# Head 1's second and third attention groups as block products, with another way of splitting the first plain weights

## The chip, the cores and the metric

The kernel runs on one core of a Trainium2 chip. The metric is the time of one execution on the device in microseconds (us). Five queues of instructions matter: TensorE (PE, matrix products, with its weight loads PEld), VectorE (DVE), ScalarE (ACT), GpSimd (POOL) and SyncE (SP). SP and POOL issue the transfers (DMAs) here.

## The reference

The reference is a trunk of two layers on a sequence of 512 tokens with 1024 channels, in float32. Layer 0 mixes tokens by attention, layer 1 by causal pooling, and each is followed by a SwiGLU network with 2816 hidden channels. The change touches the attention layer alone:

```
qkv = (rmsnorm(x) @ w_qkv).reshape(B, S, 3 groups, 3 (q, k, v), 8 heads, 128)
for g, (window, dil) in enumerate(((128, 1), (512, 4), (2048, 16))):
    o[g], lse[g] = dilated_window_attention(q[g], k[g], v[g], window, dil, slopes[g])
o = sum over g of softmax(lse over g)[g] * o[g]
x = x + o.reshape(B, S, 1024) @ w_out
```

Each head therefore needs, for each of three groups, a q and a k: two products of a 1024x128 weight with the 1024x512 normalized input.

## The kernel before, in words

**Products in split precision.** Every float32 operand is split into a high part (rounded to the type that PE takes) and a low part (what is left). A product is the sum of three: high x high, high x low, low x high. `split` (line 90) makes the two parts: ACT writes the high part (L91), then DVE subtracts it from the raw value and writes the low part (L92).

**Two kinds of product.** The plain kind (`Product`, L312, L313 and L315 in this order for each of 8 slices of the contraction) gives one 128x512 result from 24 matmuls that stream 512 columns. L315 is the one that needs the weight's low part. The block kind (`seven`, L444 to L446 inside `mult`) gives two results, q and k of a group, at once: both operands are cut into 2x2 blocks, and 7 block products take the place of 8. Each block product is 12 matmuls that stream 256 columns, so a pair takes 84. It needs sums of weight blocks (`Pair`: the raw blocks come by three transfers on SP, a fourth on POOL, L159, adds one block to two others on the way, and DVE adds twice more, L175 and L176), sums of input blocks (T), and sums of the results (L485, L493, L498, L499 on DVE).

**The input blocks T** are made by `prepare(k)` for k = 0 to 3, between the early products: two multiplications (L561), three subtractions or additions (L565, L566, L570) and four splits of 512 columns each.

**Weights and their order.** A list of loads and a list of splits are filled at the start, in the order in which the weights are used. `pump` is called after each product and takes the next load if raw tiles are free (4 of them; `prepare` takes two of them as well) and the next split if a weight tile (5 of them, each with a high and a low half) is free. So at most five split weights stand ahead of PE. The first units after the four products of the prologue (L905) are here called:

- U0, U1: q and k of group 2 of head 0;
- U2, U3: v of group 0 for heads 0 and 1;
- U4, U5: q and k of group 0 of head 1;
- U6 to U9: q and k of groups 1 and 2 of head 1.

All ten are plain in the kernel before. Heads 2 to 7 use block products throughout. After head 1's groups comes `values12` (L615 to L617), a block product for the values of groups 1 and 2.

**What stands around U0.** After the prologue's products the program computes the norm's factor: PE sums squares (L394), DVE scales (L397), POOL takes a power (L400), PE spreads the result (L407), ACT copies it out as `row` (L914). Three eighths of U0's product are written before the spread and the rest behind it. The program text is not the order in the queues: a scheduler goes through the text and gives each engine its instructions in the order in which it reckons them to be ready, earlier text first.

**Between head 1's groups.** After group 0 comes `merge` of head 0; after group 2 come `turn0`, `turn12` (transposes of head 0's weights, L782 and L803, with copies) and `scores0` of head 1 (L699).

Of the kernel before, what the change touches and what calls it, by code (L numbers as in the profile page):

```python
# [8 lines left out]
F32 = mybir.dt.float32  # L9
F32R = mybir.dt.float32r  # L10
AF = mybir.ActivationFunctionType
OP = mybir.AluOpType
# [24 lines left out]
NF = 4  # L37
# [1 line left out]
K2 = KC // 2  # L39
NPLAIN = 4  # L40
WARM = 6
NSOLO = 3
PARTS = {0: ((0, 6, False), (6, 14, True), (14, 22, True)), 1: ((0, 2, False), (2, 10, True), (10, 18, True), (18, 22, False))}
ENDS = 5
BACK = {"blocks": 3, "sums": 7}
# [14 lines left out]
QK = [(0, 0), (0, 1), (1, 0), (1, 1), (2, 0), (2, 1)]  # L60
# [4 lines left out]
def trunk(ctx: ExitStack, tc: tile.TileContext, xT, xN, norms, w_first, w_qk, w_qkp, w_v0, w_v0p, w_v12, w_out, w_pair, w_down, w_dblock, w_pin, w_pgrp,  # L65
          consts, ident_in, invcnt_in, outT, outR):
    nc = tc.nc
# [22 lines left out]
    def split(hi, lo, v):  # L90
        nc.scalar.activation(hi, v, AF.Copy)  # L91
        nc.vector.tensor_tensor(lo, v, hi.bitcast(F32), op=OP.subtract)  # L92
# [7 lines left out]
    class Held:  # L100


        def __init__(self, ring, shift=0):
            self.live = True
            n = COLS[ring]
            if ring in ("w", "half"):
                t = wpool.tile([P, 2 * n + LINE], F32R, tag=ring, name=ring, bufs=BUFS[ring])
                self.t = [t[:, shift + i * n:shift + (i + 1) * n] for i in range(2)]
            else:
                self.t = wpool.tile([P, n], F32, tag=ring, name=ring, bufs=BUFS[ring])  # L110
            rings[ring].append(self)
# [8 lines left out]
    class Plain:  # L120


        def __init__(self, *srcs, shift=0):
            self.srcs, self.n, self.w, self.shift = srcs, sum(src.shape[-1] for src in srcs), None, shift
            loads.append((self, {"raw": 1}, self.load))
            steps.append((self, "w", self.split))

# [6 lines left out]

        def split(self):
            self.w = Held("w", self.shift)
            split(*(t[:, :self.n] for t in self.w.t), self.raw.t[:, :self.n])
            self.raw.done()

    class Pair:  # L140
# [68 lines left out]
            steps.extend(parts)  # L209
        units.append((these,))  # L210

    def share(n, *srcs, shift=0):
        unit = Plain(*srcs, shift=shift)
        each = unit.n // n
        units.extend([(unit, i * each, each, i == n - 1) for i in range(n)])

# [2 lines left out]
        share(1, src[:, S:3 * S])  # L219
        share(1, src[:, 3 * S:], src[:, :S])  # L220

    def plain(*srcs):
        for src in srcs:
            share(1, src)

    for h in range(HEADS):
        if h == 0:
            plain(*[w_qk[u] for u in range(len(QK) - NF)])
        for g in range(3):
            if h == 1 and g < NSOLO:  # L230
                plain(*[w_qk[len(QK) - NF + 2 * g + c] for c in range(2)])
            elif h:
                pairs(w_qkp[3 * h - 3 - NSOLO + g])
        if h == 0:
            plain(w_v0[0], w_v0[1])
        elif h % 2 == 0:
            pairs(w_v0p[h // 2 - 1])
        else:
            pairs(w_v12[h // 2, 0], w_v12[h // 2, 1], shift=APART)
# [343 lines left out]
    with tc.tile_pool(name="opool", bufs=1) as opool:  # L583
        early = opool.tile([P, HEADS, S], F32R, tag="o", name="early")
        with tc.tile_pool(name="apool", bufs=1) as apool:
# [253 lines left out]
            H, T, o = {}, {}, []  # L839
# [46 lines left out]
            for k in range(KC):  # L886
# [15 lines left out]
                for j, (w, v) in enumerate(((hi, 0), (hi, 1), (lo, 0))):  # L902
                    for i, f in enumerate(lead):
                        c = (k % 2 * NF + i) * P
# [43 lines left out]
            for h in range(1, HEADS):  # L948
                for g in range(3):
                    if h == 1 and g < NSOLO:  # L950
                        for c in range(2):
# [58 lines left out]
    with tc.tile_pool(name="fpool", bufs=2) as fpool:  # L1010
# [326 lines left out]
        t = total(late, add(0, 1, f))  # L1337
        t = total(t, add(1, 1, end(1, 1, range(HALF))))
# [5 lines left out]
        t = total(t, add(2, 1, end(2, 1, range(HALF // 2, HALF), f)))  # L1344
# [3 lines left out]
        t = total(t, add(3, 1, f))  # L1348
# [101 lines left out]
```

## Time and profile before

| what | value |
|---|---|
| median of three runs | 1194.25 us (1193.57 to 1194.67) |
| the profiled execution's own time | 1194.79 us |
| its span, first to last instruction | 1192.6 us |
| PE busy | 1182.2 us (99%) |
| DVE busy | 995.0 us (83%) |
| ACT busy | 680.8 us (57%) |
| POOL busy | 147.5 us (12%) |
| granted PE clock | 0.998 |

The profiled execution is 0.54 us above the median. An engine's busy time counts an instruction from its start to its end; consecutive instructions of one engine may overlap a little, so the distance between two starts is often shorter than the duration given. Idle time of an engine is put down to the instruction whose end came last before it went on. In the chain that ended last, each piece is a stretch of time, so its length is the distance from one piece to the next.

### The profile page before, as it was taken

The numbers are of one execution on the slowest core, as the hardware profiler recorded it, in microseconds if no ns is written. First come the engines' busy times: TensorE is split into PE (matmuls) and PEld (weight loads), VectorE is DVE, ScalarE is ACT, GpSimd is POOL, SyncE is SP. The second block draws the span as 40 slices with busy tenths as digits, with TensorE's granted clock in tenths as the row PEclk, the third lists the DMA queues.
The fourth block names the chain that finished last, engine by engine and source line by source line (L and its number), as shares of the span: only waits on it lengthen the run. The fifth ranks groups of instructions, "written<-read, shape, count | busy, mean of one in ns | idle before, by whom it ended". The sixth has DMA issues, their size and how long they took to land.

```text
span 1192.6 us, 24834 instructions
## 1 busy us (share of the span) xinstructions
PE 1182.2 (99%) x9936; PEld 1120.0 (94%) x9936; DVE 995.0 (83%) x1712; ACT 680.8 (57%) x1214; POOL 147.5 (12%) x137
## 2 busy tenths in 40 slices
PE   9999999999999999999999999999999999999997
PEld 7889999999999988898999999998789999999997
DVE  6978898889788856795799889997989998898875
ACT  6445564555456544562677567763455776676553
POOL 1111211111111000101111111100310111111100
PEclk9999999999999999999999999999999999999999
DMA  8346656665766534336677777753153777777732
GB/s 285 118 107 159 158 152 161 171 159 149 189 146 163 158 140 126 88 110 161 160 198 190 187 200 197 192 176 124 54 123 91 192 196 200 197 187 196 193 89 71
DMA packets 73363, 188.40 MB, mean 158 GB/s; under 512 B 7312, under 2 KB 9504, under 8 KB 73248
## 3 DMA queue, kind: packets, MB, share of 16 engines
q1 hardware_dynamic: 50400, 141.98, 35.2%
q0 software_dynamic: 22704, 44.58, 23.2%
q8 instruction: 77, 1.26, 0.4%
q14 instruction: 38, 0.31, 0.1%
q10 hardware_dynamic: 144, 0.26, 0.1%
HBM read 184.70 MB, written 2.10 MB: 157 GB/s over the span
## 4 chain that ended last, share of the span: by engine, by line
PE 91%; DVE 5%; issue 2%; ACT 1%; DMA 0%; POOL 0%; DVEq 0%; POOLq 0%; SPq 0%; ACTq 0%
PE ps L444 19%; PE ps L445 18%; PE ps L446 18%; PE ps L312 7%; PE ps L313 7%; PE ps L315 7%; PE ps L615 2%; PE ps L617 2%; PE ps L616 2%; PE ps L905 2%; DVE w L92 2%; PE ps L827 1%; PE ps L699 1%; DVE far L92 1%; PE ps L821 1%
## 5 line engine op out<-in xcount | busy, mean ns | idle before, releaser
L91 ACT ACTIVATE w<-raw 128x1024 fp32r<-128x1024 f32 (+1 forms) x299 | 313.6, 1056 | 211.7 <-PE ps L446 69.0
L92 DVE TENSOR_TENSOR w<-raw,w 128x1024 fp32r<-128x1024 f32 (+1 forms) x299 | 361.7, 1214 | 59.0 <-ACT w L91 55.3
L444 PE MATMUL ps<-far,w 128*128 128x256 f32 x916 | 251.9, 275 | 0.1
L445 PE MATMUL ps<-far,w 128*128 128x256 f32 x916 | 252.0, 275 | 0.0
L446 PE MATMUL ps<-far,w 128*128 128x256 f32 x916 | 251.8, 275 | 0.0
L444 PE MATMUL ps<-near,w 128*128 128x256 f32 x632 | 178.5, 282 | 0.4 <-ACT first L526 0.4
L445 PE MATMUL ps<-near,w 128*128 128x256 f32 x632 | 174.8, 277 | 0.0
L446 PE MATMUL ps<-near,w 128*128 128x256 f32 x632 | 174.8, 277 | 0.0
L444 PEld LDWEIGHTS ps<-far,w 128*128 128x128 f32 x916 | 171.8, 188 | 0.6 <-ACT first L526 0.5
L445 PEld LDWEIGHTS ps<-far,w 128*128 128x128 f32 x916 | 172.0, 188 | 0.2
L446 PEld LDWEIGHTS ps<-far,w 128*128 128x128 f32 x916 | 172.0, 188 | 0.0
L444 PEld LDWEIGHTS ps<-near,w 128*128 128x128 f32 x632 | 118.9, 188 | 1.3 <-ACT first L526 0.9
L445 PEld LDWEIGHTS ps<-near,w 128*128 128x128 f32 x632 | 118.8, 188 | 0.0
L446 PEld LDWEIGHTS ps<-near,w 128*128 128x128 f32 x632 | 118.8, 188 | 0.0
L313 PE MATMUL ps<-near,w 128*128 128x512 f32 (+1 forms) x284 | 106.4, 375 | 1.3 <-DVE near L377 1.3
L312 PE MATMUL ps<-near,w 128*128 128x512 f32 (+1 forms) x284 | 107.0, 377 | 0.0
L315 PE MATMUL ps<-near,w 128*128 128x512 f32 (+1 forms) x284 | 106.2, 374 | 0.0
L159 POOL DMA_DIRECT2D raw<-w_pair x36 | 43.7, 1213 | 361.5 <-DMA raw<-w_pair 135.1
L313 PEld LDWEIGHTS ps<-near,w 128*128 128x128 f32 x284 | 53.4, 188 | 11.4 <-DVE near L377 2.1
L312 PEld LDWEIGHTS ps<-near,w 128*128 128x128 f32 x284 | 53.4, 188 | 9.4
L315 PEld LDWEIGHTS ps<-near,w 128*128 128x128 f32 x284 | 53.3, 188 | 9.5
L91 ACT ACTIVATE half<-rawhalf 128x512 fp32r<-128x512 f32 x81 | 51.0, 631 | 14.7 <-PE ps L446 12.5
(319 smaller groups left out, 2731.2 us busy)
## 6 DMA issues: line engine op xcount, KB each, us to landing
raw<-w_pair SPq DMA_DIRECT2D x80, 512.0 KB, 4.4
raw<-w_qkp SPq DMA_DIRECT2D x36, 512.0 KB, 4.2
raw<-w_pair POOLq DMA_DIRECT2D x36, 512.0 KB, 7.4
raw<-w_dblock SPq DMA_DIRECT2D x32, 512.0 KB, 4.3
raw<-w_v SPq DMA_DIRECT2D x18, 512.0 KB, 4.1
raw<-w_qkp POOLq DMA_DIRECT2D x18, 512.0 KB, 7.3
rawhalf<-w_pair SPq DMA_DIRECT2D x36, 256.0 KB, 5.0
raw<-w_dblock POOLq DMA_DIRECT2D x16, 512.0 KB, 7.5
```

The lines of the kernel that those rows point to most:

```text
L91: nc.scalar.activation(hi, v, AF.Copy)
L92: nc.vector.tensor_tensor(lo, v, hi.bitcast(F32), op=OP.subtract)
L159: nc.gpsimd.dma_start(self.b.rearrange("p (a c) -> p a c", a=2), self.src[:, None, 3 * n:].to_broadcast([P, 2, n]), accum_op=OP.add)
L312: nc.tensor.matmul(self.p[:, cols], w[0][:, s], mh[:, cols], start=self.done == 0, stop=False)
L313: nc.tensor.matmul(self.p[:, cols], w[0][:, s], ml[:, cols], start=False, stop=False)
L315: nc.tensor.matmul(self.p[:, cols], w[1][:, s], mh[:, cols], start=False, stop=self.done == self.n)
L444: nc.tensor.matmul(dst, w.t[0][:, c], th, start=k == 0 and not on, stop=False, skip_group_check=on)
L445: nc.tensor.matmul(dst, w.t[0][:, c], tl, start=False, stop=False, skip_group_check=on)
L446: nc.tensor.matmul(dst, w.t[1][:, c], th, start=False, stop=k == n - 1, skip_group_check=on)
L615: nc.tensor.matmul(o, mh, wh, start=k == 0, stop=False)
L616: nc.tensor.matmul(o, mh, wl, start=False, stop=False)
L617: nc.tensor.matmul(o, ml, wh, start=False, stop=k == K2 - 1)
```

## The change

Three constants and conditions are edited.

- `NSOLO` goes from 3 to 1. Of head 1, only group 0 stays a pair of plain products; groups 1 and 2 become block products (`seven`), whose weights come as two `Pair` units (here P6 and P7) in place of the plain units U6 to U9. What was written after group 2 (`turn0`, `turn12`, `scores0`) is handed to `seven`, which issues it behind its first, third and fifth block product.
- Units U0 to U5 are `lean`: ACT writes the high part as before and then its negative into the low tile, and a transfer issued by POOL adds the raw weight from memory to it. DVE has no part in these splits, and the raw tile is free once ACT has read it.
- The weights on the host's side are laid out to fit (`w_qk` shorter, `w_qkp` longer), through the same constant.

```
-NSOLO = 3
+NSOLO = 1
...
     class Plain:
-        def __init__(self, *srcs, shift=0):
-            self.srcs, self.n, self.w, self.shift = srcs, sum(src.shape[-1] for src in srcs), None, shift
+        def __init__(self, *srcs, shift=0, lean=False):
+            self.srcs, self.n, self.w, self.shift, self.lean = srcs, sum(src.shape[-1] for src in srcs), None, shift, lean
             loads.append((self, {"raw": 1}, self.load))
             steps.append((self, "w", self.split))
...
         def split(self):
             self.w = Held("w", self.shift)
-            split(*(t[:, :self.n] for t in self.w.t), self.raw.t[:, :self.n])
+            hi, lo = (t[:, :self.n] for t in self.w.t)
+            if self.lean:
+                nc.scalar.activation(hi, self.raw.t[:, :self.n], AF.Copy)
+                nc.scalar.activation(lo, hi.bitcast(F32), AF.Copy, scale=-1.0)
+                o = 0
+                for src in self.srcs:
+                    nc.gpsimd.dma_start(lo[:, o:o + src.shape[-1]], src.bitcast(F32R), accum_op=OP.add)
+                    o += src.shape[-1]
+            else:
+                split(hi, lo, self.raw.t[:, :self.n])
             self.raw.done()
...
     for h in range(HEADS):
         if h == 0:
-            plain(*[w_qk[u] for u in range(len(QK) - NF)])
+            plain(*[w_qk[u] for u in range(len(QK) - NF)], lean=True)
         for g in range(3):
             if h == 1 and g < NSOLO:
-                plain(*[w_qk[len(QK) - NF + 2 * g + c] for c in range(2)])
+                plain(*[w_qk[len(QK) - NF + 2 * g + c] for c in range(2)], lean=True)
             elif h:
                 pairs(w_qkp[3 * h - 3 - NSOLO + g])
         if h == 0:
-            plain(w_v0[0], w_v0[1])
+            plain(w_v0[0], w_v0[1], lean=True)
```

`plain` and `share` pass `lean` on. The loop that uses it stands unchanged:

```
if h == 1 and g < NSOLO:
    for c in range(2):
        evac(h, 2 * g + c, product(0))
    for fs in between(h, g).values():
        for f in fs:
            f()
else:
    ...
    seven(T, QKV[h, g, 0], QKV[h, g, 1], scratch, between(h, g), g == 0)
```

More of the change, by code (lines that the diff above doesn't have):

```diff
@@ L210, in pairs, with share @@
         units.append((these,))
-    def share(n, *srcs, shift=0):
-        unit = Plain(*srcs, shift=shift)
+    def share(n, *srcs, shift=0, lean=False):
+        unit = Plain(*srcs, shift=shift, lean=lean)
         each = unit.n // n
@@ L220, in plain_gu, with plain @@
         share(1, src[:, 3 * S:], src[:, :S])
-    def plain(*srcs):
+    def plain(*srcs, lean=False):
         for src in srcs:
-            share(1, src)
+            share(1, src, lean=lean)
     for h in range(HEADS):
         if h == 0:
-            plain(*[w_qk[u] for u in range(len(QK) - NF)])
+            plain(*[w_qk[u] for u in range(len(QK) - NF)], lean=True)
         for g in range(3):
             if h == 1 and g < NSOLO:
-                plain(*[w_qk[len(QK) - NF + 2 * g + c] for c in range(2)])
+                plain(*[w_qk[len(QK) - NF + 2 * g + c] for c in range(2)], lean=True)
             elif h:
```

## The prediction

> **What bounds the kernel now.** I read the page's first and fourth parts, then the stages by windows, then the queues around the places of the change.
>
> ```profile
> PE 1182.2 (99%) x9936; PEld 1120.0 (94%) x9936; DVE 995.0 (83%) x1712; ACT 680.8 (57%) x1214; POOL 147.5 (12%) x137
> ...
> PE 91%; DVE 5%; issue 2%; ACT 1%; DMA 0%; POOL 0%; DVEq 0%; POOLq 0%; SPq 0%; ACTq 0%
> ```
>
> PE is busy for 99% of the span and holds 91% of the chain that ended last. So PE work taken out shortens the kernel one for one, as long as no wait takes its place, and any wait put into PE's row costs its length. DVE at 83% is the engine that could become late.
>
> The stretch that is replaced, in the chain that ended last (start, length, what):
>
> ```profile
> 66.88 0.29 PE ps L312
> ...
> 88.48 0.23 PE ps L315
> 88.71 0.44 PE ps L782 x4
> ...
> 90.88 0.32 PE ps L615
> 91.20 0.12 PE ps L616
> ```
>
> Between 66.88 and 88.71 PE does nothing but the four plain products of head 1's groups 1 and 2: 96 matmuls in 21.83 us, 0.2274 us each. No wait stands in it.
>
> Three stretches by windows (from and to, length, then busy time and count for PE, PEld, DVE, ACT, POOL):
>
> ```profile
> 200.00:220.00 20.00, 20.00 (x179) 20.00 (x178) 16.34 (x21) 10.10 (x17) 1.77 (x2) 1.00 0.78 190
> 34.00:67.00 33.00, 33.00 (x267) 27.48 (x266) 30.64 (x52) 17.45 (x38) 2.41 (x2) 1.00 0.34 97
> 67.00:88.00 21.00, 21.00 (x94) 17.40 (x93) 16.84 (x33) 7.38 (x12) 3.72 (x4) 1.00 0.44 115
> ```
>
> From 200 to 220 block products run without a gap: 179 matmuls in 20 us, 0.1117 us each, with the weight loads busy all the time. From 34 to 67, just ahead of the change, DVE is busy for 30.64 of 33 us; from 67 to 88, where the plain products are, for 16.84 of 21.
>
> **The change part by part.**
>
> **Block products for groups 1 and 2.** They remove 96 long matmuls (21.83 us) and add 2 x 84 short ones: 168 x 0.1117 = 18.77 us. Gain: 3.06 us. The moved insertions (two sets of transposes and the scores) hold the same matmuls as before, but PE now goes back to products three times, not once. After the scores the first product's piece took 0.32 us where the next took 0.12, so a return costs about 0.2 us; two more cost between 0 and 0.4 us. I take 0.1, since the transposes (0.44 us for four) are more like the products than the scores are, and a row for that return is not shown. The gain is then 2.95, with ends of 2.66 and 3.06.
>
> **What DVE gets for it.** Rows of the first 300 us by shape:
>
> ```profile
> L92 DVE TENSOR_TENSOR w<-raw,w 128x1024 fp32r<-128x1024 f32 x69 | 83.7, 1221 | 15.9 <-ACT w L91 15.2
> L175 DVE TENSOR_TENSOR raw<-raw 128x512 f32<-128x512 f32 x20 | 13.7, 687 | 1.6 <-DVE w L92 1.0 <-DVE qk L499 0.5
> L176 DVE TENSOR_TENSOR raw<-raw 128x512 f32<-128x512 f32 x20 | 13.7, 685 | 0.1
> L92 DVE TENSOR_TENSOR half<-rawhalf,half 128x512 fp32r<-128x512 f32 x20 | 13.7, 685 | 0.0
> L498 DVE TENSOR_TENSOR qk<-ps,sums 128x512 f32<-128x512 f32 x12 | 8.2, 685 | 0.0
> L485 DVE TENSOR_TENSOR qk<-ps,first 128x512 f32<-128x512 f32 x12 | 8.1, 677 | 0.0
> L593 DVE TENSOR_TENSOR qk<-ps,row 128x512 f32<-128x512 f32 x12 | 8.1, 685 | 1.5 <-PE ps L315 1.4
> ...
> L493 DVE TENSOR_TENSOR sums<-ps,qk 128x512 f32<-128x512 f32 x8 | 5.5, 685 | 0.2
> L499 DVE TENSOR_TENSOR qk<-sums,ps 128x256 f32<-128x256 f32 x12 | 4.9, 412 | 0.0
> ```
>
> A block pair's weights cost DVE 3 x 1.22 + 0.69 for splits and 2 x 0.69 for additions, 5.7 us; its results cost 0.68 + 0.69 + 0.69 + 0.41 = 2.5. A plain group costs 2 x 1.22 + 2 x 0.69 = 3.8. Each exchanged group adds 4.4 us, both 8.8. The lean units take away one 1.22 each, 7.3 in all, but not where the work is added: U0 to U4 were split before 34 us, so the crowded stretch gets back U5's alone.
>
> First test, the input blocks T. The rows of DVE in order of time (U5 to U9, then the last splits of `prepare(3)`):
>
> ```profile
> 37.81 1.22 DVE L92 TENSOR_TENSOR w<-raw,w 128x1024 fp32r<-128x1024 f32 x1
> ...
> 42.29 1.23 DVE L92 TENSOR_TENSOR w<-raw,w 128x1024 fp32r<-128x1024 f32 x1
> ...
> 49.64 1.22 DVE L92 TENSOR_TENSOR w<-raw,w 128x1024 fp32r<-128x1024 f32 x1
> ...
> 55.11 1.22 DVE L92 TENSOR_TENSOR w<-raw,w 128x1024 fp32r<-128x1024 f32 x1
> ...
> 62.64 1.23 DVE L92 TENSOR_TENSOR w<-raw,w 128x1024 fp32r<-128x1024 f32 x1 [0.51 <-ACT w L91]
> ...
> 69.28 0.68 DVE L92 TENSOR_TENSOR h<-raw,h 128x512 fp32r<-128x512 f32 x1
> ...
> 72.89 0.68 DVE L92 TENSOR_TENSOR tx<-raw,tx 128x512 fp32r<-128x512 f32 x1
> ```
>
> In the kernel before T is whole at 73.57, long ahead of its first use at 90.88. Now group 1 starts near 66.9 and its fourth block product wants the last piece 45 matmuls later, at 66.88 + 45 x 0.1117 = 71.9. To be done by then, from 34 on: the 30.64 of before, less five splits (6.1), plus P6's weights (5.7), plus P7's first split (1.2), plus the part of `prepare(3)` that ran after 67 (four splits and two more operations of some 0.7 us, one multiplication, two short additions: about 5 us). That is 36.4, so the end lies at 70.4 if DVE never idles, and at 72.8 with the 2.4 us of idle time that the stretch had. The raw tiles set that idle time, and a lean unit gives its tile back after ACT instead of after DVE, so some of it should go. PE would wait between 0 and 0.9 us; with T no earlier than before, 1.7. I take 0.3, nearer the unhindered end.
>
> Second test, the stretch of both groups. From 34 to 88 DVE was busy for 47.5 of 54 us. It gets 8.8 - 1.2 more, 55.1, in a stretch that is 3 us shorter, 51. It ends some 4 us later in its list than before. What covers this is the store of weights split ahead: five tiles, each good for two block products of 12 matmuls, 5 x 24 x 0.1117 = 13.4 us of PE. Four from thirteen leaves enough, so I cost it at nothing; if that cover were already used up it would cost up to 4 us. The lag should shrink at DVE's usual 1.5 to 2 idle us in 10.
>
> **Low parts by ACT and an adding transfer.** ACT gets one more activation per lean unit, 6 x 1.06 us (as L91 below); it idles for half of this stretch, so nothing, except ahead of U0. There the order is tight. ACT, then POOL, in order of time:
>
> ```profile
> 19.24 2.07 ACT L91 ACTIVATE w<-raw 128x1024 fp32r<-128x1024 f32 x2
> ...
> 28.57 1.06 ACT L91 ACTIVATE w<-raw 128x1024 fp32r<-128x1024 f32 x1 [3.63 <-PE ps L905]
> 32.25 0.60 ACT L914 ACTIVATE row<-ps 128x512 f32<-128x512 f32 x1 [2.62 <-PE ps L407]
> ```
> ```profile
> 17.52 2.02 POOL L685 TENSOR_SCALAR b<-const 128x320 f32<-128x320 f32 x1 [17.08 <-DMA const<-consts]
> 19.52 1.45 POOL L688 TENSOR_SCALAR b<-const 128x128 f32<-128x128 f32 x2
> 29.22 2.23 POOL L400 TENSOR_TENSOR rcol<-var,nhalf 128x2 f32<-128x2 f32 x2 [8.25 <-DVE var L397]
> ```
>
> The need, in the chain:
>
> ```profile
> 28.53 0.36 PE ps L394 x32
> 28.89 0.43 PE ps L312
> 29.32 0.23 PE ps L313
> 29.55 0.23 PE ps L315
> ```
>
> And the only transfers of this kind in the trace, those of L159:
>
> ```profile
> L159 POOL DMA_DIRECT2D raw<-w_v x8: 1195/1238/1392, 57.5 to 383.1; - x8
> ...
> DMA to landing us min/median/max: 6.3/7.4/10.9
> ```
>
> U0's high part starts at 19.24; two activations of 1.06 end at 21.4, when POOL is free (19.52 + 1.45 = 20.97). The transfer lands 6.3 to 10.9 us later, at 27.7 to 32.3, median 28.8. PE wants it at 29.55. So the wait is 0 to 2.8 us; I take 0, by the median, with 0.7 to spare. [...]
>
> U1 is wanted after U0's product: five more slices (15 matmuls of 0.23) and the spread, near 36; issued 2.1 us behind U0, it lands by 34.4 even with the longest delay. U2 to U5 follow at one product of 5.5 us each and have more room. POOL's other work, one adding transfer per pair, moves back behind these. Its own pieces are 1.2 to 1.4 us of queue time each, and P6's is not wanted until some ten microseconds after it lands. The loads on SP change kind, not much in size: U6 to U9 were four of 512 KB; the two pairs are six on SP, four of that size and two of half, and two adding ones on POOL. The lean units add six transfers of 512 KB, 3 MB, mostly in a stretch where the share of the DMA engines was 0.34. I count them at nothing, since only U0 is close to its date; if that cover is gone it is the 2.8 above.
>
> **Sum.** -2.95 + 0.3 = -2.65 us. The profiled execution would go from 1194.79 to 1192.14, its span to 1189.95. The median of the runs stands 0.54 below that execution: 1194.25 - 2.65 = 1191.6 us. Own range: 2.66 less 1.7 of gain at one end (1193.3), 3.06 and a little scatter between runs at the other (1190.6).
>
> **The rivals.**
>
> *U0's low part lands late.* The longest transfer of this kind took 10.9 us. PE then waits 2.8 us: 1191.6 + 2.8 = 1194.4, no change. For it speaks that the next loads go out in the same microseconds; against it that half of these transfers took at most 7.4. [...]
>
> *DVE gets too full.* T comes as late as before (1.7 us of waiting in place of 0.3), and the lag of 4 us meets a store that is not full because pairs of the values load late: 1 to 3 us more. 1191.6 + 1.4 + 1 = 1194.0, again no change to be measured. For it: 55.1 us of work in 51. Against it: heads 2 to 7 run three such groups each, and the chain from 100 to 390 us, by line, names PE alone:
>
> ```profile
> by line: PE ps L444 23.1%; PE ps L445 22.3%; PE ps L446 22.3%; PE ps L615 5.9%; PE ps L617 5.8%; PE ps L616 5.7%; PE ps L827 3.7%; PE ps L699 2.7%; PE ps L821 1.8%; PE ps L719 1.5%; PE ps L820 1.4%; PE ps L782 0.9%; PE ps L803 0.9%; PE ps L
> ```
>
> *U0's transfer stands behind the power on POOL.* In the text the power (L400) comes ahead of U0's split. If the queue keeps that order, the transfer goes out only at 29.22 + 2.23 = 31.45 and lands, by the median, at 38.85, 9.3 us after PE wants it. This would be slower: 1194.25 - 2.95 + 9.3 = 1200.6 (T then has time). It decides from the moment that the transfer is placed behind L400, since even the shortest delay of 6.3 costs 8.2. For it: the text's order. Against it: L685 and L688, written later than L400, ran at 17.52 and 19.52, ahead of it; and on ACT two splits written behind the row (28.57 is the later) ran before it at 32.25. Queues here follow readiness.
>
> **How the numbers follow.** Within 0.2% (2.4 us) of 1194.25 is about what a measurement of this kernel can tell from no change. The forecast gets 0.56, and its own range falls mostly on the faster side; U0 late 0.12; DVE too full 0.12; the order on POOL 0.20. A part of the forecast's own range (0.03) is within 0.2%, and so are the two middle cases: faster 0.53, same 0.27, slower 0.20. The range runs from 1190.6 up through both middle cases, with the shorter end of the waits together: 1196.0.
>
> **What would show it.** Right: U0's L315 follows its L313 without a gap; 168 matmuls of L444 to L446 between some 67 and 86, at 0.112 us; `values12` starts near 88, not 90.9; the adding transfers of U0 to U3 run on POOL before L400. Wrong: a gap at PE at 29.5 with a transfer into w as its releaser (short: contention; near 9 us: the order on POOL); gaps at L444 released by DVE's tx or by w; the last tx split after 72; DVE busy without a break past 100 us and waits on w in `values12`.

## The result and the profile after

The changed kernel is slower: 1210.91 us median of four runs (1210.07 to 1213.93), against 1193.92 for the kernel before on the same chip. The ratio is 1.0144, 95% interval 1.0132 to 1.0155. The forecast was 1191.6, and the range ended at 1196.0. The profiled execution is the longest of the four (1213.93, 3.0 above the median; span 1212.1).

Behind the lean split, line numbers of the changed kernel are 9 higher: `split` keeps L91 and L92, the lean split is L139, L140 and L143, the plain product L321, L322, L324, the block products L453 to L455, the pair's transfers L165 to L168 and additions L184, L185, `values12` L624 to L626, the row L923. Two lines of the page, busy time by engine and the chain that ended last:

```profile
PE 1187.3 (98%) x10008; PEld 1126.3 (93%) x10008; DVE 995.4 (82%) x1718; ACT 689.8 (57%) x1226; POOL 155.4 (13%) x145
...
PE 87%; DVE 6%; DMA 3%; issue 2%; ACT 1%; SPq 0%; POOL 0%; DVEq 0%; POOLq 0%; ACTq 0%
```

The count of matmuls is as worked out (9936 + 168 - 96 = 10008). But PE is busy for 5.1 us more, not less, and a transfer now stands in the chain. The list of PE's waits by what ended them:

```profile
PE ps L681 <- DVE vt L602: 7.9, 2, 5.3
PE ps L732 <- DVE qk L507: 3.1, 1, 3.1
PE ps L324 <- DMA w<-w_qk: 1.6, 1, 1.6
```

The columns are the sum, the count and the longest, in us. None of these three is in the kernel before. Three stations show where the loss arises. The row starts at 35.66 (before 32.25). The first matmul of `values12` starts at 104.0 (90.8), and the first in which `output` of head 0 takes the values of groups 1 and 2 (L836, before L827) at 135.0 (115.9). From there on the loss hardly grows (19.1 us there, 19.5 at the end). So 3.4 us are lost ahead of the row, 9.8 more up to `values12` in spite of what the block products gain, and 5.9 in `values12`.

The windows of the kernel after, with columns as in the prediction (the last three are granted clock, DMA share and GB/s):

```profile
20.00:30.00 10.00, 9.63 (x72) 7.42 (x71) 1.82 (x4) 8.62 (x10) 5.37 (x8) 1.00 0.88 232
30.00:40.00 10.00, 8.75 (x35) 7.39 (x36) 2.01 (x3) 1.39 (x2) 2.85 (x4) 0.83 1.05 262
...
50.00:60.00 10.00, 8.26 (x152) 6.96 (x149) 10.00 (x17) 5.45 (x8) 0.00 (x0) 1.00 0.51 106
60.00:70.00 10.00, 3.43 (x13) 2.81 (x14) 10.00 (x19) 4.80 (x13) 2.52 (x2) 0.63 0.58 133
70.00:80.00 10.00, 10.00 (x40) 8.09 (x39) 7.21 (x14) 4.80 (x10) 0.00 (x0) 0.86 0.00 0
...
110.00:120.00 10.00, 9.07 (x83) 9.04 (x84) 6.09 (x12) 5.42 (x16) 1.24 (x1) 0.66 0.62 141
```

and the first two of these windows in the kernel before:

```profile
20.00:30.00 10.00, 10.00 (x75) 8.09 (x74) 6.60 (x9) 4.49 (x5) 1.67 (x4) 1.00 0.78 244
30.00:40.00 10.00, 10.00 (x49) 8.33 (x48) 8.01 (x12) 3.85 (x6) 1.44 (x1) 1.00 0.21 79
```

Between 30 and 40 the DMA engines go from a share of 0.21 to 1.05, and DVE from 8.0 busy us to 2.0. DVE then has no idle moment from 50 to 70, and there PE waits. Why DVE stood still is read from three queues of the kernel after. SP (issue of the second pair's last load; the first pair's went out at 25.91), ACT and DVE, in order of time:

```profile
27.13 0.46 SPq L167 DMA_DIRECT2D rawhalf<-w_qkp  x1
```
```profile
35.66 0.60 ACT L923 ACTIVATE row<-ps 128x512 f32<-128x512 f32 x1 [4.87 <-PE ps L416]
41.79 0.63 ACT L91 ACTIVATE half<-rawhalf 128x512 fp32r<-128x512 f32 x1 [5.53 <-DMA rawhalf<-w_qkp]
...
45.23 0.63 ACT L91 ACTIVATE half<-rawhalf 128x512 fp32r<-128x512 f32 x1 [2.29 <-DMA rawhalf<-w_qkp]
```
```profile
42.97 0.69 DVE L92 TENSOR_TENSOR near<-raw,near 128x512 fp32r<-128x512 f32 x1 [4.67 <-ACT near L91]
...
47.02 1.28 DVE L602 TENSOR_TENSOR qk<-ps,row 128x512 f32<-128x512 f32 x2
```

ACT's queue holds the split of the first pair's last load (`half`) right behind the row, ahead of the split of an input block (`near`). The load has not landed, so ACT stands for 5.5 us; DVE, whose next instruction is that block's low part, stands behind ACT, with a product's result waiting behind it in turn. The same happens with the second pair. The chain says how long that second load took:

```profile
27.13 18.07 DMA rawhalf<-w_qkp
```

18.07 us for 256 KB. In the kernel before, the first two pairs are those of `values12`. The splits of their last loads stood at the same place in ACT's queue, right behind the row, and waited for nothing (the first):

```profile
32.74 0.62 ACT L91 ACTIVATE half<-rawhalf 128x512 fp32r<-128x512 f32 x1
```

What the load had to share the engines with are the lean units' transfers. POOL's queue of the kernel after, and the time from issue to landing over the six of L143:

```profile
21.85 1.05 POOL L143 DMA_DIRECT2D w<-w_qk  x1 [0.74 <-DVE sq L376]
23.87 0.87 POOL L143 DMA_DIRECT2D w<-w_qk  x1 [0.96 <-ACT w L140]
26.69 1.80 POOL L143 DMA_DIRECT2D w<-w_v  x2 [1.96 <-ACT w L140]
29.29 1.40 POOL L409 TENSOR_TENSOR rcol<-var,nhalf 128x2 f32<-128x2 f32 x2 [0.79 <-DVE var L406]
```
```profile
DMA to landing us min/median/max: 5.5/11.4/14.3
```

Later the same pattern comes back with `w_v`, the weights of `values12`. ACT, DVE and PE of the kernel after:

```profile
95.55 1.06 ACT L91 ACTIVATE w<-raw 128x1024 fp32r<-128x1024 f32 x1 [3.46 <-DMA raw<-w_v]
```
```profile
96.65 1.23 DVE L92 TENSOR_TENSOR w<-raw,w 128x1024 fp32r<-128x1024 f32 x1 [3.19 <-ACT w L91]
```
```profile
110.93 0.68 PE L732 MATMUL ps<-qk,qk 128*32 128x32 f32 x32 [3.10 <-DVE qk L507]
```

PE waits there for results that DVE has not finished, in the middle of `values12`. A further cost comes with the waits. Windows of one us, PE alone (busy, granted clock, DMA share, GB/s), around the first wait:

```profile
31.00:32.00 1.00, 0.75 (x3) 0.91 1.07 279
32.00:33.00 1.00, 1.00 (x4) 0.50 1.02 254
...
35.00:36.00 1.00, 1.00 (x8) 0.89 1.06 274
```

After PE's wait the granted clock is 0.50 for some 3.4 us, in which PE does about half of its work: about 1.7 us on top of the wait. (Between 69 and 72 us, at 0.50, the matmuls of a plain product start 0.43 us apart; at 1.00 it is 0.23.) It happens again between 60 and 80 and between 110 and 120: by the windows above, 10 x (0.37 + 0.14) / 0.5 = 10.2 us and 10 x 0.34 / 0.5 = 6.8 us at half clock, three and two times 3.4. Part of the first of these stretches is the second wait itself.

### The profile page after: what moved, and what is told of

Same layout as the page of the kernel before. It is cut to its first block, busy times and chain, and to the rows that moved or that the text cites. A ratio compares the mean times of both kernels' runs of the same rounds, so it can differ in the third digit from the quotient of the medians.

```text
span 1212.1 us, 25035 instructions
## 1 busy us (share of the span) xinstructions
PE 1187.3 (98%) x10008; PEld 1126.3 (93%) x10008; DVE 995.4 (82%) x1718; ACT 689.8 (57%) x1226; POOL 155.4 (13%) x145
## 4 chain that ended last, share of the span: by engine, by line
PE 87%; DVE 6%; DMA 3%; issue 2%; ACT 1%; SPq 0%; POOL 0%; DVEq 0%; POOLq 0%; ACTq 0%
PE ps L453 19%; PE ps L454 18%; PE ps L455 18%; PE ps L321 7%; PE ps L322 7%; PE ps L324 7%; PE ps L624 2%; PE ps L625 2%; PE ps L626 2%; DMA rawhalf<-w_qkp 1%; DVE w L92 1%; PE ps L836 1%; DMA raw<-w_dblock 1%; PE ps L708 1%; PE ps L830 1%
## 5 line engine op out<-in xcount | busy, mean ns | idle before, releaser
L91 ACT ACTIVATE w<-raw 128x1024 fp32r<-128x1024 f32 (+1 forms) x295 | 309.6, 1056 | 207.2 <-PE ps L455 67.8
L92 DVE TENSOR_TENSOR w<-raw,w 128x1024 fp32r<-128x1024 f32 (+1 forms) x295 | 357.3, 1215 | 62.4 <-ACT w L91 59.0
L453 PE MATMUL ps<-far,w 128*128 128x256 f32 x916 | 252.0, 275 | 0.1
L455 PE MATMUL ps<-far,w 128*128 128x256 f32 x916 | 251.9, 275 | 0.0
L453 PE MATMUL ps<-near,w 128*128 128x256 f32 x664 | 187.7, 283 | 0.6 <-ACT first L535 0.6
L454 PE MATMUL ps<-near,w 128*128 128x256 f32 x664 | 183.7, 277 | 0.0
L455 PE MATMUL ps<-near,w 128*128 128x256 f32 x664 | 183.6, 277 | 0.0
L453 PEld LDWEIGHTS ps<-far,w 128*128 128x128 f32 x916 | 171.8, 188 | 0.8 <-ACT first L535 0.5
L455 PEld LDWEIGHTS ps<-far,w 128*128 128x128 f32 x916 | 171.9, 188 | 0.0
L453 PEld LDWEIGHTS ps<-near,w 128*128 128x128 f32 x664 | 125.0, 188 | 1.6 <-ACT first L535 1.2
L454 PEld LDWEIGHTS ps<-near,w 128*128 128x128 f32 x664 | 124.8, 188 | 0.0
L455 PEld LDWEIGHTS ps<-near,w 128*128 128x128 f32 x664 | 124.8, 188 | 0.0
L322 PE MATMUL ps<-near,w 128*128 128x512 f32 (+1 forms) x284 | 106.4, 375 | 1.4 <-DVE near L386 1.4
L321 PE MATMUL ps<-near,w 128*128 128x512 f32 (+1 forms) x284 | 107.2, 377 | 0.1
L324 PE MATMUL ps<-near,w 128*128 128x512 f32 (+1 forms) x284 | 106.3, 374 | 0.0
L168 POOL DMA_DIRECT2D raw<-w_pair x36 | 43.6, 1212 | 360.1 <-DMA raw<-w_pair 140.3
L91 ACT ACTIVATE half<-rawhalf 128x512 fp32r<-128x512 f32 x83 | 52.2, 630 | 22.1 <-PE ps L455 12.1
L322 PEld LDWEIGHTS ps<-near,w 128*128 128x128 f32 x284 | 53.4, 188 | 11.4 <-DVE near L386 2.1
L321 PEld LDWEIGHTS ps<-near,w 128*128 128x128 f32 x284 | 53.4, 188 | 9.8 <-ACT near L385 0.5
L324 PEld LDWEIGHTS ps<-near,w 128*128 128x128 f32 x284 | 53.3, 188 | 9.6
```

The costliest lines, as they stand in the source:

```text
L168: nc.gpsimd.dma_start(self.b.rearrange("p (a c) -> p a c", a=2), self.src[:, None, 3 * n:].to_broadcast([P, 2, n]), accum_op=OP.add)
L321: nc.tensor.matmul(self.p[:, cols], w[0][:, s], mh[:, cols], start=self.done == 0, stop=False)
L322: nc.tensor.matmul(self.p[:, cols], w[0][:, s], ml[:, cols], start=False, stop=False)
L324: nc.tensor.matmul(self.p[:, cols], w[1][:, s], mh[:, cols], start=False, stop=self.done == self.n)
L453: nc.tensor.matmul(dst, w.t[0][:, c], th, start=k == 0 and not on, stop=False, skip_group_check=on)
L454: nc.tensor.matmul(dst, w.t[0][:, c], tl, start=False, stop=False, skip_group_check=on)
```

## The experiments

The theories. **A, transfers and queue**: the adding transfers fill the DMA engines (share 1.05 from 30 to 40), the pairs' last loads land late (18.07 us), and the queues of ACT and DVE stand behind them (5.53 and 4.67 us in the rows above). **B, DVE's work**: the added 8.8 us make DVE late wherever PE takes a result from it at once. **C, the half clock** lengthens each wait. The change is first cut into its two parts, then single causes are taken out. Where two kernels were timed on different chips, each is compared with the kernel before on its own chip.

### The lean splits alone

```
-NSOLO = 1
+NSOLO = 3
```

> The lean splits alone: head 1's groups all stay plain products (so ten units, U0 to U9, are lean). Theory A (the adding transfers crowd the DMA engines, loads come late, and ACT's queue is held behind a split that waits for one of them): clearly slower than before, by 8 us or more, with ACT waiting several us for a rawhalf load near 36 us and the DMA engines full from 22 to 45 us. Theory B (the block products give DVE more than it can do in head 1): no slower than before by more than 1 us, since no block product was added. Theory C (only the wait for U0's low part and the lower clock behind it): slower by 3 to 4 us.

With `NSOLO` back at 3, U6 to U9 are plain units again and so lean as well: ten adding transfers, where the change has six.

Measured: 1202.27 us (1199.66 to 1203.55) against 1194.67, ratio 1.0060 (1.0045 to 1.0075). PE's two new waits in its profiled execution (the fastest, 1199.66), and ACT right behind the row:

```profile
31.67 0.50 PE L324 MATMUL ps<-early,w 128*128 128x512 f32 x1 [2.94 <-DMA w<-w_qk]
61.18 0.66 PE L681 MATMUL ps<-ident,vt 128*128 128x128 f32 x4 [2.02 <-DVE vt L602]
```
```profile
43.60 0.63 ACT L91 ACTIVATE half<-rawhalf 128x512 fp32r<-128x512 f32 x1 [6.93 <-DMA rawhalf<-w_v]
```

The lean splits, meant to relieve DVE, cost 7.6 us by themselves, without a block product in head 1. Theory A had 8 us or more, and its sign is there: ACT stands 6.9 us for the last load of a pair, here one of `values12`.

### The block products alone

```
-            plain(*[w_qk[u] for u in range(len(QK) - NF)], lean=True)
+            plain(*[w_qk[u] for u in range(len(QK) - NF)])
...
```

> The block products alone: all splits by ACT and DVE as before, groups 1 and 2 of head 1 as block products. Theory A: no wait of more than 1 us near 30 us, loads land in 5 us, and the time lies between 1190.5 and 1196 (the 3 us gained, less what DVE comes late). Theory B: 8 us or more slower than before. Theory C: about 1191.

Measured: 1197.96 us (ten runs, 1195.73 to 1199.67) against 1194.67, ratio 1.0022 (1.0012 to 1.0032). Slower by 3.3 where the prediction had the matmuls give 3.06 less; none of the three theories had forecast this size. The two parts add up to 10.9 of the 17.0 lost, so there is an interplay. It does not lie in the hold of ACT: that is about as long with the lean splits alone (6.9 us, against 5.5 and 2.3 in the changed kernel), and yet PE waits 2.0 us for `vt` there and 7.9 in the changed kernel. In the changed kernel DVE has splits of weights (53.22 and 58.64) and additions for the pairs (61.89 and 64.69) to do ahead of `vt`; with the lean splits alone it has none of these between 50 and 61. That this work makes the difference was not tested by itself. POOL, DVE and PE of this kernel at its longest wait:

```profile
71.88 1.20 POOL L168 DMA_DIRECT2D raw<-w_v  x1 [17.03 <-DMA raw<-w_v]
```
```profile
80.68 0.69 DVE L184 TENSOR_TENSOR raw<-raw 128x512 f32<-128x512 f32 x1 [1.62 <-DMA raw<-w_v]
81.29 0.94 DVE L775 TENSOR_SCALAR s<-s,co 128x160 f32<-128x160 f32 x4
```
```profile
82.37 0.63 PE L791 MATMUL ps<-ident,s 128*128 128x128 f32 x4 [2.42 <-DVE s L775]
```

DVE's queue stands behind a weight addition whose transfer is under way, and the scaled scores that `turn0` needs stand behind that. So theory A's queue is at work without a lean unit, too: DVE's lag frees raw tiles late, the next loads go out late (that of L168 at 71.88), and DVE's queue reaches their use 1.62 us before they land. A block product's own matmuls are also less short than was reckoned (see the steps below).

### The first unit plain

```
-            plain(*[w_qk[u] for u in range(len(QK) - NF)], lean=True)
+            plain(w_qk[0])
+            plain(w_qk[1], lean=True)
```

> The changed kernel, but U0 is split by ACT and DVE as before; U1 to U5 stay lean. Theory C (U0's wait and the lower clock behind it are what costs) says that most of the 17 us goes: below 1198. Theory A (ACT held behind the pairs' third loads) says that U0's own wait of 1.6 us and the 1.7 us that PE loses at half clock behind it go, and a little of the hold, since one transfer of six is gone: 1203 to 1208, with ACT still held by rawhalf for several us.

Measured: 1208.96 us (1207.27 to 1212.34) against 1194.28, ratio 1.0127 (1.0111 to 1.0142). The wait for U0's low part is gone, which is worth about 2 us; the 7.6 us of waits for DVE's `vt` stay. The time is a little above theory A's 1203 to 1208 and far above the 1198 of theory C. So the wait that the prediction had watched is the small one.

### The pairs' last splits held back

The splits of the first two pairs' `half` take a scale that DVE writes after the first value product, so ACT's queue cannot have them at its head before that. All transfers stay.

```
+                nc.scalar.activation(hi, self.c, AF.Copy, scale=one_late[0])
+                nc.vector.tensor_tensor(lo, self.c, hi.bitcast(F32), op=OP.subtract)
...
+                    nc.vector.tensor_scalar(one_late[0], p[:, :1], 0.0, 1.0, op0=OP.mult, op1=OP.add)
```

> The changed kernel with all its transfers, but the last splits of P6 and P7 on ACT take their factor (1.0) from a tile that is written only after the first value product, so they can't stand ahead of the splits of the input blocks. Theory A: the DMA engines are as full as in the changed kernel, yet ACT no longer waits for rawhalf near 36 us, the splits of the input blocks start by 38, PE's waits for the value tiles near 61 to 67 are gone, and the time is 1195 to 1200 (U0's wait stays). Theory B and theory C: 1208 to 1213, as the changed kernel.

Measured: 1200.33 us (1199.41 to 1202.42) against 1194.67, ratio 1.0049 (1.0034 to 1.0064). Of the 17.0 us lost 5.7 are left: 11.3 less, by moving two activations and two subtractions in their queues. PE's waits that are left are 1.0 (U0), 1.0 (`vt`), 0.8 (in `merge`) and one of 3.0 in `values12`:

```profile
PE ps L742 <- ACT s L727: 3.0, 1, 3.0
```

### The transfers made small

Each adding transfer moves 128 of 1024 columns, so most of the low parts of U0 to U5 are not right in it. Queues and instructions stay.

```
-                    nc.gpsimd.dma_start(lo[:, o:o + src.shape[-1]], src.bitcast(F32R), accum_op=OP.add)
+                    nc.gpsimd.dma_start(lo[:, o:o + P], src[:, :P].bitcast(F32R), accum_op=OP.add)
```

> The changed kernel with all its instructions in their places, but each adding transfer of a lean unit moves 128 of its 1024 columns (so the low parts of U0 to U5 are left wrong; the time is that of the same work with an eighth of the added bytes). Theory A: the wait for U0's low part is under 1 us, the third loads of the pairs land before ACT wants them, and the time is between 1190 and 1196. Theory B: still above 1204, since DVE has the same work. Theory C: about 1191 to 1193.

Measured: 1198.45 us (1197.5 to 1200.7) against 1194.67, ratio 1.0033 (1.0020 to 1.0046). Of the 17.0 us 3.8 are left, 13.2 less, and the splits of `half` stand at their old place in ACT's queue without a wait (the second one):

```profile
34.15 0.62 ACT L91 ACTIVATE half<-rawhalf 128x512 fp32r<-128x512 f32 x1
```

Together with the one before this settles the large part: neither the transfers alone (held splits) nor the queue's order alone (small transfers) costs the 11 to 13 us; it takes both. The time is still 2.5 us above the 1196 that theory A allowed: PE waits 3.2 us for DVE in `values12` (L732), as in the changed kernel.

### Head 1's second scores later

The held splits, and `scores12` of head 1 behind the third block product of `values12` instead of the first.

```
-                    QKV[h // 2, 12, 2] = values12({0: [later(scores12, h)], 4: [later(scatter, h)]})
+                    QKV[h // 2, 12, 2] = values12({2 if h == 1 else 0: [later(scores12, h)], 4: [later(scatter, h)]})
```

> The kernel of e4_held_splits, and head 1's second scores, on which PE waited 3 us for DVE and ran at half clock after it, stand behind the third block product of the values in place of the first. If DVE's lag is what PE waits for there, the wait goes and 4 to 5 us with it: 1195 to 1197. If the wait only moves to the next place where PE needs DVE, the time stays at 1199 to 1201.

Measured: 1196.30 us (ten runs, 1195.81 to 1198.29) against 1194.28, ratio 1.0022 (1.0012 to 1.0031). Between the second and the third station above `values12` takes 25.0 us again (before 25.1, held splits 29.5). So a wait of 3.0 us cost 4.5 there. Theory B's place is right: the lag meets PE where it takes a result that DVE has just been given.

### Is the difference the half clock?

The held splits, with 18 idle matmuls of 128 columns just ahead of that wait, so that PE does not stand.

```
+                if h == 1:
+                    fill = ps()
+                    for r in range(18):
+                        nc.tensor.matmul(blk(fill, r % NT), blk(QKV[h, 1, 0], r % NT), blk(QKV[h, 1, 1], r % NT), start=True, stop=True)
```

> The kernel of e4_held_splits, with 18 idle 128x128 products (about 0.22 us each) on PE where it waits 3 us for DVE ahead of the second part of head 1's second scores; their results are not used. The wait itself is filled, not removed. If the lower clock behind a wait costs time of its own, the granted clock stays at 1.00 from 90 to 120 us and the time falls by 1 to 2 us against e4_held_splits, to about 1198.5 to 1199.5. If only the wait costs, the time stays or rises by up to 1 us: 1200 to 1201.5.

Measured: 1199.89 us (1199.63 to 1202.41) against 1194.43, ratio 1.0051 (1.0038 to 1.0065), the same as without. The clock stays at 1.00 where it fell to 0.50 for 3 us, but the fill took 4.0 us in place of the 3.0 waited, and `values12` takes 29.0 us in place of 29.5. So the fill costs its own length and nothing on top (29.0 against 25.0), where the wait of 3.0 cost 4.5. In the whole time this is too small a difference to tell the two forecasts apart.

### More moves

The held splits with U0 plain, and the interludes between head 1's products spread out: value transposes of head 0 behind the next product, its merge into group 1, `turn0`, `turn12` and `scores0` behind the third, fourth and sixth block product, `scores12` as above.

```
+                    a, b, c = (2, 3, 5) if h == 1 else (0, 2, 4)
+                    return {a: [later(turn0, h - 1)], b: [later(turn12, h - 1)], c: [later(scores0, h)]}
...
```

> Block products, lean splits without U0, the last splits held back as in e4_held_splits, and every place where PE took something from DVE in head 1 moved back by some block products (the value transposes, the merge, the two turns, both scores). If waits on late results are all that stands between the change and its gain, no wait of 0.5 us is left between 28 and 120 us and the time is 1191 to 1193. If DVE's work in this stretch is too much in itself, PE waits on weights or on evacuations instead, and the time is 1194 to 1198.

Measured: 1193.68 us (eleven runs, 1192.04 to 1196.35) against 1194.28, ratio 0.9995 (0.9987 to 1.0004): no difference. It is the best kernel here that computes everything. One wait over 0.4 us of those that the kernel before does not have is left (0.5, `turn0`).

The same moves without lean units and without the held splits:

> The same places moved, and all splits by ACT and DVE as before (no adding transfers). If the lean units' relief of DVE is not needed, it equals e8_spread within 1 us, 1191 to 1193. If it is needed, DVE falls 6 us further behind and PE waits: 1194 to 1198.

Measured: 1196.88 us (nine runs, 1196.29 to 1198.67) against 1194.28, ratio 1.0022 (1.0013 to 1.0032). `turn0` waits 3.5 us. And with `turn0`, `turn12`, `scores0` and `scores12` all moved into `values12`:

> No lean units; the two turns of head 0 and both scores of head 1 stand behind block products of the values, so that nothing in head 1's groups takes a result of DVE but the value transposes (moved behind a product) and the merge. If e9_spread_no_lean was slow only by the 3.5 us that PE waited at the first turn, the time is 1191 to 1193.5. If DVE's work is too much in itself, a wait of 2 us or more shows up later, at the values' evacuations or scores, and the time is 1194 to 1198.

Measured: 1195.05 us (eleven runs, 1194.73 to 1196.92) against 1194.43, ratio 1.0010 (1.0001 to 1.0019). This one with U4 and U5 lean:

> As e11_turns_later, and U4 and U5 lean (two adding transfers in place of six, of which U5's alone takes work from DVE where it is busy). If DVE's load decides, it is 1 to 2 us faster than e11_turns_later; if two transfers already disturb ACT's queue, slower than it by 1 us or more; else equal within 0.7.

Measured: 1194.44 us (eleven runs, 1193.31 to 1196.69) against 1194.43, ratio 1.0000 (0.9991 to 1.0009). In both, DVE still stands behind the addition for `w_v`, and PE meets the lag at the next place. DVE with U4 and U5 plain, and PE's waits in the same kernel:

```profile
82.82 0.69 DVE L184 TENSOR_TENSOR raw<-raw 128x512 f32<-128x512 f32 x1 [3.37 <-DMA raw<-w_v]
```
```profile
PE ps L836 <- DVE v L665: 1.9, 1, 1.9
```

So moving PE's insertions only moves the wait on.

### DVE relieved

The block products alone, with the low parts of U4, U5 and of `b`, `s` and `m` of both pairs written by ACT as scaled copies. These eight low parts are not right; eight subtractions of 1.22 us, 9.8 us of DVE's work, are gone, and no adding transfer is added.

```
+            elif len(rings["w"]) in (9, 10):
+                nc.scalar.activation(hi, self.raw.t[:, :self.n], AF.Copy)
+                nc.scalar.activation(lo, hi.bitcast(F32), AF.Copy, scale=2.0 ** -13)
...
```

> The kernel of e2_blocks_only, where DVE leaves out the low parts of U4, U5, P6 and P7 (some 11 us of its work between 29 and 90 us); ACT writes a scaled copy of the high part there instead, so that these low parts are wrong and the time is that of the same work with a less loaded DVE and no adding transfers. If DVE's load in this stretch is what takes the block products' gain, no wait of 0.5 us is left on PE from 28 to 130 us and the time is 1191 to 1192.5. If something else does (the order of the queues, the raw tiles), it stays near e2_blocks_only, 1195 to 1199.

Measured: 1191.36 us (ten runs, 1190.46 to 1193.35) against 1194.51, ratio 0.9975 (0.9966 to 0.9985). The gain is 3.15 us, with the interval from 1.8 to 4.1, where 3.06 were worked out for the matmuls. The windows of the prediction in this kernel, and in the one with the block products alone:

```profile
34.00:67.00 33.00, 33.00 (x270) 27.61 (x270) 31.29 (x59) 26.42 (x49) 3.55 (x2) 1.00 0.40 99
67.00:88.00 21.00, 21.00 (x258) 20.83 (x257) 17.36 (x38) 13.47 (x25) 3.35 (x4) 1.00 0.67 162
```
```profile
34.00:67.00 33.00, 31.54 (x259) 26.07 (x258) 32.81 (x58) 17.68 (x39) 2.27 (x2) 1.00 0.37 81
67.00:88.00 21.00, 18.58 (x141) 18.17 (x140) 19.06 (x42) 11.32 (x23) 3.51 (x4) 0.92 0.62 151
```

DVE has 1.7 us to spare in the first window (31.29 of 33, in place of 32.81), and PE is full in both. The first adding transfer for `w_v` goes out at 67.46 in place of 71.88. This confirms theory B for what the block products alone lose. Of a lag of DVE itself and of raw tiles that it gives back late, the kernel takes away both at once, so it does not tell their shares apart.

### The same relief with all values computed

The block products alone, with the subtractions of eight (then five) of these low parts on POOL, which with the block products alone is busy for 2.27 of the 33 us from 34 to 67.

```
-        nc.vector.tensor_tensor(lo, v, hi.bitcast(F32), op=OP.subtract)
+        (engine or nc.vector).tensor_tensor(lo, v, hi.bitcast(F32), op=OP.subtract)
...
```

> The blocks alone with every value computed: eight low parts (U4, U5, and the b, s and m of P6 and P7) are subtracted by GpSimd instead of VectorE, with no added transfer. If VectorE's load is the cause of the lost gain: VectorE is relieved of about 11 us as in e13, and if GpSimd takes about 3.3 us for a subtraction of 1024 columns (from its 1625 ns for 512) the eight take 26 us beside 30 to 86 us of the span, so that 1191.0 to 1192.8. If GpSimd's slower subtraction becomes the new lag, its values come behind their date, TensorE waits at a weight of U5 or P6 by 2 us or more, and the time is 1194 to 1199.

Measured: 1199.6 us (1198.72 to 1201.11) against 1194.32, ratio 1.0046 (1.0034 to 1.0059).

> The same with five low parts (U5, and the b and s of P6 and P7), about 7 us less on VectorE. VectorE's load as the cause: 1191.5 to 1194, a smaller lag than in e2 but not none; if GpSimd's lateness decides, this one is faster than the one with eight; if VectorE's load decides, slower than it.

Measured: 1202.33 us (1201.9 to 1203.14) against 1194.32, ratio 1.0069 (1.0055 to 1.0082).

Both are slower than with every subtraction on DVE. Eight moved is better than five, as a relieved DVE would have it, but both times lie far outside what that theory had forecast; and PE waits for `vt` (4.7 and 4.5 us) and for scores, not for the weights that a late POOL would hold back. POOL and DVE of the kernel with eight show why no relief arrives:

```profile
42.71 2.43 POOL L92 TENSOR_TENSOR w<-raw,w 128x1024 fp32r<-128x1024 f32 x1 [4.29 <-ACT w L91]
50.45 2.40 POOL L92 TENSOR_TENSOR w<-raw,w 128x1024 fp32r<-128x1024 f32 x1 [5.32 <-ACT w L91]
```
```profile
41.52 0.75 DVE L573 SCALAR_TENSOR_TENSOR raw<-x,nrm,row 128x512 f32<-128x512 f32 x1
...
42.79 2.90 DVE L573 SCALAR_TENSOR_TENSOR raw<-x,nrm,row 128x512 f32<-128x512 f32 x1
...
50.48 0.88 DVE L714 SCALAR_TENSOR_TENSOR s<-ps,b 128x480 f32<-128x480 f32 x2
51.28 2.12 DVE L186 TENSOR_TENSOR raw<-raw 128x512 f32<-128x512 f32 x1
```

The same DVE operation (L573) takes 0.75 us, and 2.90 when it falls into POOL's subtraction; it ends about half a us behind POOL's. L186, 0.69 elsewhere, takes 2.12 and ends 0.55 behind POOL's. L714, which reads a product's result (`ps`), took 0.88 beside POOL, as it did in the kernel before (0.88). So the 1.22 us of DVE's work that each moved subtraction takes away came back here as 2.15 and 1.43, beside POOL's subtractions of 2.43 and 2.40. The rows show how much longer these two operations took, not by what. Why five moved are worse than eight is not settled.

## Why the prediction was wrong, by its steps

**Block products for groups 1 and 2: the mechanism right, the term too large.** From the first product of group 1 to the first matmul of `values12` PE needed 24.1 us before (66.69 to 90.81, starts of matmuls). With DVE relieved it is:

```profile
66.14 0.36 PE L464 MATMUL ps<-near,w 128*128 128x256 f32 x1
```
```profile
88.11 0.28 PE L635 MATMUL ps<-w,near 128*128 128x256 f32 x1
```

That is 22.0 us, a gain of 2.15; in the changed kernel the stretch takes 21.6 us, a gain of 2.5, and with the late scores 22.2, a gain of 1.95. PE waits for nothing in any of them. The forecast was 2.95, with 2.66 as its lower end. The count of 179 in a window of 20 us takes in matmuls that lie in it only in part; from start to start the short ones are 0.113 us apart, and in a part of these stretches 0.118, where 0.1117 was taken. The first behind each insertion takes 0.2, so that the returns of PE cost something too. That the kernel with DVE relieved is 3.15 us faster as a whole, close to 3.06, is therefore in part luck: in its trace 0.55 us of that are gained ahead of the stretch.

**"The lean units add six transfers of 512 KB, 3 MB, mostly in a stretch where the share of the DMA engines was 0.34. I count them at nothing, since only U0 is close to its date": wrong, and the largest error.** Four of the six were issued between 21.85 and 27.6. From 20 to 30 the share had been 0.78 in the kernel before already, and it went to 0.88, and to 1.05 in the next 10 us; the 0.34 was that of 34 to 67. What was late, apart from U0's 1.6 us, was none of these units but loads of another kind that shared the engines, and these are not wanted by PE until long after. Their consumer, ACT's split, stood early in ACT's queue with the input blocks behind it, and ACT stood there for 5.53 us. The rows of that queue in the kernel before (32.74) showed the place. Making the transfers small gave back 13.2 us, and holding the splits back 11.3. The prediction asked when PE wants each transfer, not which instruction stands behind it in each queue.

**"The crowded stretch gets back U5's alone": right, and it shows why the lean splits could pay little.** They take DVE's work mostly from where DVE had time. That they are of no use is not shown: of the two kernels with the same moves, the one with lean and held splits is 3.2 us faster than the one with neither.

**U0's low part: a miss in the term, inside its bounds.** It was taken at 0, with ends 0 and 2.8; the wait was 1.62 (2.94 with lean splits alone). The median of 7.4 came from transfers issued one at a time; queued behind each other they took up to 14.3. The half clock was not priced: U0 and it together put the row back by 3.4 us.

**The order on POOL: right to reject as the likeliest.** U0 to U3 went out before the power (L409), at 21.85 to 27.6. The chance of a slower kernel had been hung on this rival; the slower result came by another way.

**First test, the input blocks: 0.3 taken, ends 0 to 1.7.** With block products alone the last `tx` split ended near 69.7, a little ahead of the forecast's 70.4 to 72.8, and PE did not wait for it.

**Second test, "what covers this is the store of weights split ahead ... so I cost it at nothing": wrong.** The prediction reckoned a lag of 4 us and named 4 us as the price without cover. The cover protects products that use weights. PE also takes scores and scaled scores from DVE almost at once, and these have no store. Moreover the lag holds raw tiles, so the weights load late: DVE stood 1.62 us for `w_v` while it was already behind. Block products alone lost 3.3 where 2.65 was to be gained, 6.0 off; 3.9 of it are PE's waits of 2.4 and 1.5, and some 1.7 of the rest is the half clock for 3.4 us after the longer one (the short matmuls from 83.1 to 86.3 are 0.21 us apart). What is left is about what the block products' gain was short. With DVE relieved the waits are gone.

**Not in the list at all: the half clock after a wait.** It turned the wait of 3.0 us in `values12` into 4.5.

What stays open: with the held splits and the late scores, PE's new waits make 2.9 us and the block products gain 1.95 by the rows, yet the kernel is 2.0 slower, not 0.95. No wait in the list explains the other 1.1 us. Nor was it found out why the short matmuls go at 0.113 us in some stretches and at 0.118 in others. Nor was a complete kernel found that beats the one before.

## What to carry to other kernels

When a change adds transfers, look at the DMA share in the few microseconds in which they run, list every load that shares that time, and then for each the queue in which its first user stands and what is behind it; the date on which the matrix engine wants the data is not the date that counts. A lag of an engine is only covered by stores for the things that have a store: look for the results that are taken from it at once, and for the buffers that it gives back late. Work moved off a full engine helps only if it leaves the full stretch and if the first engine's own operations do not take longer beside it, as DVE's did here (2.90 us in place of 0.75).

## What the runs showed of the hardware

**Half clock after waits.** In the changed kernel the granted clock fell to 0.50 after PE's wait of 1.62, in the wait of 5.27 that stands closely behind one of 2.67, and after the wait of 3.10. It also fell in or after those of 2.94 (lean splits alone), 2.42 (block products alone), 3.00 (held splits), 3.22 (small transfers) and 4.7 (eight on POOL). It did not fall after 1.93 (eight on POOL), 2.02 (lean splits alone) and, with U0 plain, 3.30. So between 1.6 and 3.3 us the length alone doesn't decide. In the changed kernel the slow stretches last 3.41 us (from 31.83), 10.24 (from 62.55) and 6.83 (from 110.34), and the six changes of the clock lie 3.41, 27.31, 10.24, 37.55 and 6.83 us apart: 1, 8, 3, 11 and 2 times 3.413.

Two waits of about the same length lay differently against such steps. The wait of 3.10 in the changed kernel lay mostly in the last 3.41 us before the fall, which have 0.92 us of work and 2.49 of idle time:

```profile
106.91:110.32 3.41, 0.92 (x9) 1.00 0.74 210
```

The wait of 3.30 with U0 plain was shared out between two stretches, cut in steps of 3.413 us from the first change of the clock in that trace on, and the clock stayed at 1.00:

```profile
103.49:106.90 3.41, 1.47 (x14) 1.00 0.69 224
106.90:110.31 3.41, 2.05 (x45) 1.00 1.02 166
```

That the place of a wait decides is what these two suggest; it was not tested by itself.

**The price of adding transfers.** The page's row of the queue that carries them, before and after:

```profile
q0 software_dynamic: 22704, 44.58, 23.2%
```
```profile
q0 software_dynamic: 24112, 48.77, 24.8%
```

Eight more transfers, 4.19 MB, took 0.248 x 1212.1 - 0.232 x 1192.6 = 23.9 us of all 16 engines, about 3.0 us each. When four of them went out within 6 us beside the pairs' loads, a load of 256 KB took 18.07 us from its issue to its landing.
